# Query products of a hybrid mLSTM and MLA step: rotary parts of four heads in two row-matched tiles, the query norm as a factor per token, sample products last

## The chip, the cores and the metric

The kernel runs on one core of a Trainium2 chip. The metric is the device time of one execution in microseconds (us). Runs of a kernel are compared by the median of their times; beside them stands one execution taken by the hardware profiler, from which all durations below come. Five engines work side by side, each through its own queue of instructions: TensorE (PE, with its weight loads shown as PEld), VectorE (DVE), ScalarE (ACT), GpSimd (POOL) and SyncE (SP, which here only issues DMAs). They meet at semaphores.

## The reference

One step of a decoder trunk of two layers, for 1024 prompt tokens and 8 sample tokens that see 8192 cached positions. Layer 0 mixes with an mLSTM, layer 1 with multi-head latent attention (MLA), and each is followed by a SwiGLU FFN. The change lies in the queries of the MLA layer and in the softmax of its prompt:

```python
c_q, c_kv, k_r = jnp.split(x @ w_in, [Q_LORA, Q_LORA + KV_LORA], axis=-1)
q = (rmsnorm(c_q, g_q) @ w_uq).reshape(B, S, MLA_HEADS, QK_NOPE + QK_ROPE)
q_nope = q[..., :QK_NOPE]                 # 128 of a head's 192 columns
q_rope = rope(q[..., QK_NOPE:], pos)      # the other 64
...
x1, x2 = x32[..., : d // 2], x32[..., d // 2:]
rope = [x1 * cos - x2 * sin, x1 * sin + x2 * cos]
...
s = (scores of q with the keys) * MLA_SCALE
p = jax.nn.softmax(masked s, axis=-1)
```

There are 8 heads, Q_LORA is 384, and x is already multiplied with the RMS factor of the layer's norm. So two factors per token stand in a query: that of the layer's norm (rs in the kernel) and that of the query norm (rq).

## The kernel before, in words

The 1032 tokens lie in the free dimension, in three chunks of 344 (CW); features lie on the partitions. A product in near-float32 precision is three matmuls of "high" and "low" parts (mm3, L131 to L133): high by high, high by low, low by high. So every operand is split (L114, L115): ACT makes the high part, DVE or POOL subtracts it from the source and leaves the low part. Weights come through the pool wp, two buffers each of wr (raw), wh and wl; their high and low parts are lines L114 and L115 too, with the tile names wh and wl. Results of products lie in PSUM tiles sc (four banks) and mm (two); a head's three chunks use sc, sc, mm.

The projections (L1160 on) give c_q in ev_q (L1179 to L1184): DVE multiplies the PSUM tile with rs (L1182, tile cf), ACT squares it for the query norm, and ACT and DVE split it, with g_q as pointer scale, into cqh and cql. rs_of(rq, QL) (L1249) turns the sum of squares into a row of factors over all 128 partitions, with matmuls at L229 and L235, a Newton iteration on DVE and copies on ACT. Then rc, the cosines, and rn, the sines with signs, are multiplied with rq (L1251 on POOL, L1252 on DVE).

queries() follows an order written out by hand, the string ORDER. In it "P3" is plain(3), the 128 unrotated columns of head 3: 27 matmuls over three chunks, each chunk multiplied with rq on DVE (L1334, tile qf), split into qx (the middle chunk's low part on POOL), stored to qn_d by SP (L1339), its eight sample columns copied to qnS (L1341). "R4" is rotary(4), the 64 rotary columns of heads 4 and 5 side by side: 27 matmuls, and ACT copies the result to ra (L1308); then four DMAs on ACT's queue (L1312) write rb, which is ra with the halves of each head exchanged. "t4" is rotate(4): ra times rc on POOL (L1320), rb times rn on DVE (L1321), the sum on DVE (L1322), high parts on ACT (L1325), low parts on DVE (L1326), a store to qr_d per head, and the sample columns to qrS (L1329). "A0" lets the first block of the prompt's attention start. After all of them sample_query() makes sixteen small products of qnS with the absorbed key weights wT (L1377; float32, two records each in the trace).

A scheduler then places all instructions of all engines by data and by its own estimate of when they are ready, and fixes one order per engine, so that neighbouring steps mix: the sample products stand wherever the scheduler found room. Stores of one step are issued when the next has been written.

attention() reads a block's queries back (q from qn_d, qrr from qr_d), and each head's weights w_uk and w_uv as spl (split to swh and swl by ACT and DVE). For a block, PE makes the scores (L1495 to L1502), DVE takes the maximum (L1503) and multiplies it with -SCALE (L1506, L1508), ACT takes the exponential with that as bias and SCALE as a constant scale (L1511), and the rest of the softmax and the products follow. Between prompt blocks stand sixteen units of the samples' attention over the gathered cache (nat and nrp, by POOL).

Of the kernel before, what the change touches and what calls it, by code (L numbers as in the profile page):

```python
# [48 lines left out]
ORDER = "R0 P0 P1 R2 P2 t0 R4 P3 t2 P4 R6 P5 t4 P6 P7 t6 A0"  # L49
# [6 lines left out]
def host_tables():  # L56
    p = np.arange(P)
    c = np.zeros((P, C_END), np.float32)
    c[:, C_ID:C_ID + P] = np.eye(P)
    c[:, C_MM:C_MM + P] = np.where(p[:, None] <= p[None, :], 0.0, BIG)  # L60
    c[:, C_MA:C_MA + P] = np.where(p[None, :] <= p[:, None], 0.0, -BIG)
    c[:, C_SL:C_SL + P] = (p[:, None] % 8) == (p[None, :] % 8)
    c[:, C_MC:C_MC + 2] = (p[:, None] // 64) == np.arange(2)[None, :]
    c[:, C_PM] = p % 16
    c[:, C_L8] = p < 8
    c[:, C_QS:C_QS + 4] = p[:, None] == 32 * np.arange(4)[None, :]
    h = np.arange(8)
# [8 lines left out]
    r = np.stack([np.concatenate([cos, cos, cos, cos]), np.concatenate([-sin, sin, -sin, sin])], 1)  # L76
    return c, r.astype(np.float32)
# [11 lines left out]
class Kern:  # L89
# [39 lines left out]
    def mm3(self, ps, wh, wl, xh, xl, start, stop, **kw):  # L129
        mm = self.nc.tensor.matmul  # L130
        mm(ps, wh, xh, start=start, stop=False, **kw)  # L131
        mm(ps, wh, xl, start=False, stop=False, **kw)  # L132
        return mm(ps, wl, xh, start=False, stop=stop, **kw)  # L133
# [105 lines left out]
    def rms_tok(self, SS, n):  # L239
        nc = self.nc  # L240
        c, rem = divmod(n, P)
        ps = self.tp()
        for i in range(c):
            nc.tensor.matmul(ps[:, i:i + 1], SS[:, i * P:(i + 1) * P], self.ones[:, 0:1], start=True, stop=True)
        v = self.t(self.gp, [P, 9], "tv")
        w = c + (rem > 0)
        if rem:
            nc.gpsimd.memset(v[:, c:w], 1.0)
            nc.tensor.matmul(ps[:rem, c:w], SS[:, c * P:n], self.ones[:, 0:1], start=True, stop=True)
            nc.vector.tensor_scalar(v[:rem, c:w], ps[:rem, c:w], 1.0 / D, EPS, op0=ALU.mult, op1=ALU.add)  # L250
        nc.vector.tensor_scalar(v[:, :c], ps[:, :c], 1.0 / D, EPS, op0=ALU.mult, op1=ALU.add)
        return self.rsqrt(self.gp, v[:, :w], [P, 9], "t", w)
# [856 lines left out]
    def to_mla(self, wd, fs):  # L1109
# [29 lines left out]
        self.as_row(y, rs, T)  # L1139
        return z, rs  # L1140


    def mla(self, z, rs):
# [17 lines left out]
        rq = self.t(cqp, [P, T], "rq")  # L1161
# [4 lines left out]
        rtab = self.t(mt, [P, T], "rtab")  # L1166
# [102 lines left out]
        z = self.attention(ckh, ckl, kk, kl, cqp, (cqh, cql, rc, rn, rq, wT))  # L1269
# [17 lines left out]
    def queries(self, qs, cq):  # L1287
        nc = self.nc
        V = nc.vector
        cqh, cql, rc, rn, rq, wT = cq  # L1290
# [12 lines left out]
        def rotary(h):  # L1303
            ra = self.t(qs, [P, T], "ra", bufs=2)
            rb = self.t(qs, [P, T], "rb", bufs=2)

            def ev(c, cs, ps):
                nc.scalar.copy(ra[:, cs], ps)  # L1308

            self.linear(weights([(i * 64, (h + i) * 192 + P, 64) for i in range(2)]), (cqh, cql), 3, P, ev)  # L1310
            for i in range(4):
                nc.scalar.dma_start(rb[i * 32:i * 32 + 32], ra[(i ^ 1) * 32:(i ^ 1) * 32 + 32])  # L1312
            return ra, rb

        def rotate(h, ra, rb):
            x = [self.t(qs, [P, S], f"qr{i}", F32R, bufs=1) for i in range(2)]
            for c in range(NCH):
                cs = slice(c * CW, (c + 1) * CW)
                w = slice(c * CW, min((c + 1) * CW, S))
                nc.gpsimd.tensor_tensor(ra[:, cs], ra[:, cs], rc[:, cs], op=ALU.mult)  # L1320
                V.tensor_tensor(rb[:, cs], rb[:, cs], rn[:, cs], op=ALU.mult)  # L1321
                V.tensor_tensor(ra[:, cs], ra[:, cs], rb[:, cs], op=ALU.add)  # L1322
                for i in range(2):
                    me, ot = slice(i * 64, i * 64 + 64), slice(64 - i * 64, 128 - i * 64)
                    nc.scalar.activation(x[i][me, w], ra[me, w], AF.Copy)  # L1325
                    V.tensor_tensor(x[i][ot, w], ra[me, w], x[i][me, w].bitcast(F32), op=ALU.subtract)  # L1326
            for i in range(2):
                stores.append(lambda i=i: nc.sync.dma_start(self.qr_d[h + i], x[i].bitcast(F32)))
                V.tensor_copy(self.qrS[:, h + i], ra[i * 64:i * 64 + 64, S:])  # L1329

        def plain(h):
            def ev(c, cs, ps):
                f = self.t(qs, [P, CW], "qf", bufs=3)
                V.tensor_tensor(f, ps, rq[:, cs], op=ALU.mult)  # L1334
# [3 lines left out]
                self.split(x[:, 0], x[:, 1], f[:, :n], lo_eng=nc.gpsimd if c == 1 else None)  # L1338
                stores.append(lambda: nc.sync.dma_start(self.qn_d[h, :, :, w].rearrange("i p s -> p i s"), x.bitcast(F32)))  # L1339
                if n < CW:  # L1340
                    V.tensor_copy(self.qnS[:, h], f[:, n:])  # L1341
# [3 lines left out]
        rot = {}  # L1345
        stores = []
        for op in ORDER.split():
# [56 lines left out]
    def attention(self, ckh, ckl, kk, kl, cqp, cq):  # L1404
# [70 lines left out]
        def prompt(h, G, kt, vt):  # L1475
# [5 lines left out]
            for i in (2 * G, 2 * G + 1):  # L1481
# [8 lines left out]
                for c in range(nb):  # L1490
# [13 lines left out]
                    sc.append((o, ks))  # L1504
                if nb == 2:
                    V.tensor_scalar(mx[:, 0:1], mx[:, 0:1], mx[:, 1:2], -SCALE, op0=ALU.max, op1=ALU.mult)  # L1506
                else:
                    V.tensor_scalar(mx[:, 0:1], mx[:, 0:1], -SCALE, None, op0=ALU.mult)  # L1508
                px = self.t(self.wp, [P, 1024], "wr")
                for c, (o, ks) in enumerate(sc):  # L1510
                    nc.scalar.activation(px[:, ks], o, AF.Exp, bias=mx[:, 0:1], scale=SCALE, accum_out=sm[:, c:c + 1])  # L1511
# [52 lines left out]
        self.sample_query(qs, cq[-1])  # L1564
# [305 lines left out]
```

## Time and profile before

| | us |
|---|---|
| runs | 2786.38, 2792.11, 2802.57 |
| median | 2792.11 |
| the profiled execution | 2765.05 |
| its span, first to last instruction | 2763.3 |
| mean granted PE clock | 0.971 |

In the span, mLSTM, its FFN and the MLA projections come first; the first query product (cqh by wh) starts at 1319.65, the last ends near 1402.5, attention runs until about 1905, and the output projection and the second FFN fill the rest. A row of the profile's groups gives line, engine, operation, output and inputs with their shapes and the count; behind the first bar busy time in us and mean ns of one; behind the second the engine's idle time before these instructions, and what ended it. A row of the waits gives the waiting engine, tile and line, what it waited for, then total us, number of times and the longest. A row of the stretches gives for each engine its busy us and in brackets its instructions, then the granted PE clock, the share of the DMA engines' time, and GB/s. A row of the chain has start, length and what ran.

### The profile page before, as it was taken

Reading aid. Unit: us, or ns where it says so; the run is one execution under the profiler, and the core shown is the slowest. Engines: PE = TensorE matmul, PEld = TensorE weight load, DVE = VectorE, ACT = ScalarE, POOL = GpSimd, SP = SyncE. Lnnn points to the kernel's source line nnn. Section 1 sums busy time; section 2 is a strip of 40 time slices with the busy share of each in tenths; the row PEclk is TensorE's granted clock in tenths of the full one; section 3 lists DMA queues with packets and bytes.
Section 4 is the critical chain, followed back from the end, with each engine's and each line's share of the span. In section 5 each row is a group of like instructions: output and inputs, shape, how many; then the busy total and the mean of one; then the engine's idle time right before and its main releaser. Section 6 shows DMA issues by size and latency. Waiting matters only on the chain.

```text
span 2763.3 us, 52062 instructions
## 1 busy us (share of the span) xinstructions
PE 2587.8 (94%) x20715; PEld 2438.1 (88%) x20715; DVE 1523.6 (55%) x3230; ACT 1181.6 (43%) x2687; POOL 875.2 (32%) x823
## 2 busy tenths in 40 slices
PE   8999998989999999999978878888989999999998
PEld 8998877989999999999866666767888999999998
DVE  4345578863334434465768767676574434434455
ACT  4212334544444444453455544545344444444442
POOL 1001002242333333332335544432223333333333
PEclk9999989999999999999989999998999999999999
DMA  5133455426655565451667765553533655555552
GB/s 184 39 76 92 128 147 134 131 71 126 127 117 117 115 125 116 93 173 54 190 230 272 255 228 194 200 198 119 165 100 90 128 114 123 119 115 117 116 140 100
DMA packets 344346, 378.45 MB, mean 137 GB/s; under 512 B 24250, under 2 KB 297023, under 8 KB 335783
## 3 DMA queue, kind: packets, MB, share of 16 engines
q0 software_dynamic: 37328, 170.42, 26.0%
q1 hardware_dynamic: 289494, 192.07, 23.3%
q10 hardware_dynamic: 17280, 12.64, 2.0%
q8 instruction: 162, 2.65, 0.4%
q14 instruction: 82, 0.66, 0.1%
HBM read 251.44 MB, written 121.51 MB: 135 GB/s over the span
## 4 chain that ended last, share of the span: by engine, by line
PE 66%; DVE 12%; DMA 10%; issue 5%; ACT 4%; POOL 2%; SPq 0%; ACTq 0%; POOLq 0%; DVEq 0%
PE sc L133 10%; PE sc L131 10%; PE sc L132 10%; PE mm L131 5%; PE mm L132 5%; PE mm L133 5%; PE ss L131 5%; PE ss L132 5%; PE ss L133 5%; DMA Gb<-G_d 2%; DVE tt L1648 2%; DVE wl L115 1%; PE ss L1680 1%; DMA nrp<-in_cache_k_rope_dram,idx 1%; PE mm L1552 1%
## 5 line engine op out<-in xcount | busy, mean ns | idle before, releaser
L131 PE MATMUL ss<-ah,dh 128*128 128x344 f32 x864 | 277.1, 321 | 5.9 <-ACT st L1071 5.5
L1071 ACT COPY st<-ss 128x344 f32<-128x344 f32 x432 | 190.0, 441 | 213.3 <-PE ss L133 181.6
L132 PE MATMUL ss<-al,dh 128*128 128x344 f32 x864 | 277.1, 321 | 1.9 <-POOL al L115 1.9
L133 PE MATMUL ss<-ah,dl 128*128 128x344 f32 x864 | 276.4, 320 | 0.0
L114 ACT ACTIVATE wh<-wr 128x512 fp32r<-128x512 f32 (+2 forms) x157 | 126.3, 806 | 230.9 <-PE mm L132 132.6
L1073 POOL DMA_DIRECT2D x_d<-st x144 | 125.2, 869 | 238.4 <-ACT st L1071 235.6
L131 PEld LDWEIGHTS ss<-ah,dh 128*128 128x128 f32 x864 | 162.7, 188 | 6.9 <-ACT st L1071 6.0
L115 POOL TENSOR_TENSOR al<-u,ah 128x512 fp32r<-128x512 f32 (+1 forms) x84 | 118.4, 1410 | 148.5 <-ACT ah L114 148.3
L132 PEld LDWEIGHTS ss<-al,dh 128*128 128x128 f32 x864 | 163.1, 189 | 2.4 <-POOL al L115 2.4
L115 DVE TENSOR_TENSOR wl<-S,wl 128x512 fp32r<-128x512 f32 x89 | 78.0, 877 | 156.9 <-ACT wl L114 122.5
L133 PEld LDWEIGHTS ss<-ah,dl 128*128 128x128 f32 x864 | 162.7, 188 | 0.0
L1648 DVE STREAM_TRANSPOSE tt<-nat 128x1024 f32<-128x1024 f32 x128 | 153.3, 1220 | 16.6 <-PE ss L1655 11.7
L115 DVE TENSOR_TENSOR wh<-S,wh 128x512 fp32r<-128x512 f32 x91 | 68.2, 749 | 120.3 <-ACT wh L114 91.7
L1037 DVE TENSOR_TENSOR u<-u,sc 128x260 f32<-128x260 f32 (+1 forms) x168 | 70.8, 421 | 114.0 <-PE sc L133 112.7
L115 DVE TENSOR_TENSOR wl<-wr,wh 128x1024 fp32r<-128x1024 f32 (+2 forms) x88 | 101.4, 1154 | 31.6 <-ACT wh L114 31.3
L1003 POOL TENSOR_TENSOR S<-S,wr 128x512 f32<-128x512 f32 x45 | 62.9, 1397 | 176.4 <-DVE wl L115 88.4
L996 POOL TENSOR_TENSOR S<-wr 128x512 f32<-128x512 f32 x45 | 62.3, 1385 | 164.8 <-DMA wr<-in_ffn_w_gate_up_dram 159.3
L131 PE MATMUL mm<-zh,wh 128*128 128x344 f32 x320 | 105.3, 329 | 9.1 <-DVE ot L455 9.1
L115 DVE TENSOR_TENSOR dl<-dr,dh 128x256 fp32r<-128x256 f32 x144 | 67.9, 472 | 71.5 <-ACT dh L114 71.5
L132 PE MATMUL mm<-zl,wh 128*128 128x344 f32 x320 | 104.5, 327 | 0.0
L133 PE MATMUL mm<-zh,wl 128*128 128x344 f32 x320 | 104.3, 326 | 0.0
L1005 POOL TENSOR_TENSOR S<-S,wr 128x512 f32<-128x512 f32 x45 | 58.0, 1289 | 129.8 <-DVE wh L115 83.7
(904 smaller groups left out, 9313.5 us busy)
## 6 DMA issues: line engine op xcount, KB each, us to landing
x_d<-st POOLq DMA_DIRECT2D x144, 516.0 KB, 5.5
wr<-in_ffn_w_gate_up_dram SPq DMA_DIRECT2D x98, 512.0 KB
dr<-in_ffn_w_down_dram SPq DMA_DIRECT2D x144, 128.0 KB
wr<-in_mlstm_w_in_dram SPq DMA_DIRECT2D x24, 512.0 KB
wr<-in_mlstm_w_out_dram SPq DMA_DIRECT2D x16, 512.0 KB
q<-qn_d SPq DMA_DIRECT2D x32, 256.0 KB
wr<-in_mla_w_o_dram SPq DMA_DIRECT2D x15, 512.0 KB
qn_d<-qx SPq DMA_DIRECT2D x16, 344.0 KB
```

The lines of the kernel that those rows point to most:

```text
L114: ins = nc.scalar.activation(hi, src, AF.Copy)
L115: self.low = e.tensor_tensor(lo, src, hi.bitcast(F32), op=ALU.subtract)
L131: mm(ps, wh, xh, start=start, stop=False, **kw)
L132: mm(ps, wh, xl, start=False, stop=False, **kw)
L133: return mm(ps, wl, xh, start=False, stop=stop, **kw)
L996: G(s, a21, a22, op=ALU.add)
L1003: G(s, s, a11, op=ALU.subtract)
L1005: G(s, s, a12, op=ALU.subtract)
L1037: V.tensor_tensor(u[:, 1], u[:, 1], ps, op=ALU.add)
L1071: nc.scalar.copy(st[:, cs], ps)
L1073: nc.gpsimd.dma_start(self.x_d[:, d], st, accum_op=ALU.add)
L1648: V.transpose(out=tt, in_=src.rearrange("p s (c i) -> p c s i", i=32))
```

## The change

The query norm's factor isn't applied to the queries of the prompt at all. ev_q splits and squares the PSUM tile directly, without rs. From the sum of squares rms_tok makes, with the layer's factor y, one factor per token in the layout "token on the partition" (rqt, times SCALE and times -SCALE). That is where the softmax needs it: the pointer of the maximum's product and of the exponential's scale takes rqt in place of the constants. For the sample columns, rqS holds the factors as a row, and each evacuation multiplies its eight columns with it.

rotary(h0) now makes four heads at once. Its weights are split so that one product tile holds the first rotary halves of the four heads (32 rows each), and the other the second halves; so x1 and x2 of one head and frequency are in the same row of two tiles, and cosine and sine need no exchange of rows: four multiplications on DVE out of PSUM, a subtraction and an addition on POOL, and the split. The tiles rfa and rfb between them have two buffers. rotate() and its DMAs are gone, the stores to qr_d carry four heads of 32 rows. plain() splits its PSUM tile directly, with all low parts on DVE. ORDER becomes shorter, and sample_query is placed after the last query product. The core of the diff:

```diff
-ORDER = "R0 P0 P1 R2 P2 t0 R4 P3 t2 P4 R6 P5 t4 P6 P7 t6 A0"
+ORDER = "R0 P0 P1 R4 P2 P3 P4 P5 P6 P7 A0"
...
-    def rms_tok(self, SS, n):
+    def rms_tok(self, SS, n, m=D, f=None):
...
+        if f is not None:
+            nc.vector.tensor_tensor(v[:, :w], v[:, :w], f, op=ALU.mult)
+            nc.vector.tensor_scalar(v[:, :w], v[:, :w], EPS, None, op0=ALU.add)
...
-                f = self.t(mt, [P, CW], "cf", bufs=3)
-                V.tensor_tensor(f, ps, rs[:, cs], op=ALU.mult)
-                self.squares(rq[:, cs], f, j == 0)
-                self.split(cqh[:, j, cs], cql[:, j, cs], f, self.gcol(self.G_Q + j))
+                self.split(cqh[:, j, cs], cql[:, j, cs], ps, self.gcol(self.G_Q + j))
+                self.squares(rq[:, cs], ps, j == 0)
...
-        self.rs_of(rq, QL)
-        nc.gpsimd.tensor_tensor(rc, rc, rq, op=ALU.mult)
-        V.tensor_tensor(rn, rn, rq, op=ALU.mult)
+        V.tensor_tensor(y2, self.ry, self.ry, op=ALU.mult)
+        y = self.rms_tok(rq, T, QL, y2)
+        V.tensor_tensor(y, y, self.ry, op=ALU.mult)
+        ps = self.tp()
+        nc.tensor.matmul(ps[:, :NS], y[:, 8:9].to_broadcast([P, P]), self.ident[:, :NS], start=True, stop=True)
+        self.rqS = self.t(p2, [P, NS], "rqS")
+        V.tensor_copy(self.rqS, ps[:, :NS])
+        self.rqt = self.t(p2, [P, 2, 8], "rqt")
+        for i in range(2):
+            V.tensor_scalar(self.rqt[:, i], y[:, 0:8], (SCALE, -SCALE)[i], None, op0=ALU.mult)
...
+        def rotary(h0):
+            raw = self.t(self.wp, [P, KT * P], "wr")[:, : 3 * 256].rearrange("p (k c) -> p k c", c=256)
             for i in range(4):
-                nc.scalar.dma_start(rb[i * 32:i * 32 + 32], ra[(i ^ 1) * 32:(i ^ 1) * 32 + 32])
-            return ra, rb
+                nc.sync.dma_start(raw[:, :, i * 64:i * 64 + 64], self.wsrc(wuq, 0, 3, (h0 + i) * 192 + P, 64))
...
+                for e in range(2):
+                    ps.append(self.mmt(("sc", "mm")[e])[:, :CW])
+                    for k in range(3):
+                        self.mm3(ps[e], wh[:, e, k], wl[:, e, k], cqh[:, k, cs], cql[:, k, cs], k == 0, k == 2)
+                for e, (x, y) in enumerate(((rc, rn), (rn, rc))):
+                    f, g = (self.t(qs, [P, CW], "rf" + i, bufs=2) for i in "ab")
+                    V.tensor_tensor(f, ps[0], x[:, cs], op=ALU.mult)
+                    V.tensor_tensor(g, ps[1], y[:, cs], op=ALU.mult)
+                    nc.gpsimd.tensor_tensor(f, f, g, op=(ALU.subtract, ALU.add)[e])
+                    self.split(out[e][0][:, w], out[e][1][:, w], f[:, :n])
...
         def plain(h):
             def ev(c, cs, ps):
-                f = self.t(qs, [P, CW], "qf", bufs=3)
-                V.tensor_tensor(f, ps, rq[:, cs], op=ALU.mult)
...
-                self.split(x[:, 0], x[:, 1], f[:, :n], lo_eng=nc.gpsimd if c == 1 else None)
+                self.split(x[:, 0], x[:, 1], ps[:, :n])
...
-                    V.tensor_copy(self.qnS[:, h], f[:, n:])
+                    V.tensor_tensor(self.qnS[:, h], ps[:, n:], self.rqS, op=ALU.mult)
...
-                    nc.scalar.activation(px[:, ks], o, AF.Exp, bias=mx[:, 0:1], scale=SCALE, accum_out=sm[:, c:c + 1])
+                    nc.scalar.activation(px[:, ks], o, AF.Exp, bias=mx[:, 0:1], scale=f, accum_out=sm[:, c:c + 1])
...
-        self.sample_query(qs, cq[-1])
+        with self.tc.issue_after(self.lastq.ins):
+            self.sample_query(qs, cq[-1])
```

How the instructions stand on the engines is the scheduler's result. Three places matter.

ACT around the rotary parts of heads 4 and 5. Before, the high parts of a rotation (qr), the copies of the next pair (ra) and the DMAs that swap its halves (rb) stand between the weights' high parts (wh, L114 from wr) and those of plain heads (qx):

```order
1140 L1325 ACTIVATE qr_14786<-ra_14557 64x336
1141 L1308 COPY ra_14686<-sc_14706 128x344
1142 L1325 ACTIVATE qr_14787<-ra_14557 64x336
1143 L114 ACTIVATE wh_14816<-wr_14814 128x384
1144 L1308 COPY ra_14686<-mm_14717 128x344
1145 L1312 DMA rb_14687<-ra_14686 32x1032 x4
1146 L114 ACTIVATE qx_14752<-qf_14750 128x344
```

After, at heads 4 to 7, r0h and r1h are the high parts of the first and the second rotary halves, out of the POOL sums rfa:

```order
1119 L114 ACTIVATE qx_14612<-mm_14602 128x336
1120 L114 ACTIVATE r0h_14630<-rfa_14655 128x344
1121 L114 ACTIVATE r1h_14632<-rfa_14662 128x344
1122 L114 ACTIVATE r0h_14630<-rfa_14689 128x344
1123 L114 ACTIVATE r1h_14632<-rfa_14696 128x344
1124 L114 ACTIVATE r0h_14630<-rfa_14723 128x336
1125 L114 ACTIVATE qx_14766<-sc_14756 128x344
1126 L114 ACTIVATE wh_14802<-wr_14800 128x384
```

The copies to ra and the DMAs have left ACT's queue, and plain heads' high parts read PSUM (sc, mm) in place of qf.

DVE at the same place. Before, the low parts of two weights (wl) stand ahead of a rotation, whose products (rb), sums (ra) and low parts (qr) follow:

```order
1482 L115 TENSOR_TENSOR wl_14692<-wr_14688,wh_14691 128x384
1483 L115 TENSOR_TENSOR wl_14737<-wr_14734,wh_14736 128x384
1484 L1321 TENSOR_TENSOR rb_14558<-rb_14558,rn_13611 128x344 x2
1485 L1322 TENSOR_TENSOR ra_14557<-ra_14557,rb_14558 128x344 x2
1486 L1321 TENSOR_TENSOR rb_14558<-rb_14558,rn_13611 128x344
1487 L1326 TENSOR_TENSOR qr_14786<-ra_14557,qr_14786 64x344
1488 L1326 TENSOR_TENSOR qr_14787<-ra_14557,qr_14787 64x344
```

After, the end of heads 4 to 7 (rfa, rfb, r0l, r1l), with the first chunks of P2 (qx_14766, qx_14779) and the low part of P3's weights (wl_14803):

```order
1497 L1338 TENSOR_TENSOR rfb_14732<-mm_14713,rc_13612 128x344
1498 L115 TENSOR_TENSOR r0l_14631<-rfa_14723,r0h_14630 128x336
1499 L1342 TENSOR_TENSOR rs_14634<-rfa_14723,rqS_14259 128x8
1500 L115 TENSOR_TENSOR qx_14766<-sc_14756,qx_14766 128x344
1501 L1342 TENSOR_TENSOR rs_14634<-rfa_14731,rqS_14259 128x8
1502 L1348 COPY qrS_14391<-rs_14634 32x8 x4
1503 L115 TENSOR_TENSOR r1l_14633<-rfa_14731,r1h_14632 128x336
1504 L1348 COPY qrS_14391<-rs_14634 32x8 x4
1505 L115 TENSOR_TENSOR qx_14779<-sc_14769,qx_14779 128x344
1506 L115 TENSOR_TENSOR wl_14803<-wr_14800,wh_14802 128x384
```

The low part of P3's weights stands behind the last low part of the four heads' rotation; before, the next weights' low parts stood ahead of a pair's rotation.

PE at the sample products (L1377 before, L1392 after). Before, one of them stands between two query heads, with four more places like it, and the last ten behind the scores of the first attention blocks:

```order
8497 L132 MATMUL mm_14538<-cql_13609,wh_14504 128x344
8498 L133 MATMUL mm_14538<-cqh_13608,wl_14505 128x344
8499 L1377 MATMUL ss_15194<-qnS_14402,wT_13613 128x8
8500 L131 MATMUL sc_14566<-cqh_13608,wh_14562 128x344
8501 L132 MATMUL sc_14566<-cql_13609,wh_14562 128x344
```

After, all sixteen stand behind the scores of the first blocks:

```order
8749 L1513 MATMUL sc_15066<-kk_13597,qrr_15046 128x256
8750 L1515 MATMUL sc_15066<-kl_13598,qrr_15046 128x256
8751 L1517 MATMUL sc_15066<-mk_14379 128x128
8752 L1392 MATMUL ss_15106<-qnS_14390,wT_13614 128x8 x16
8753 L1510 MATMUL sc_15211<-kt_14290,q_15205 128x384
```

On PE nothing of the samples stands between query products any more. The scheduler's order of the attention stage that follows differs from before in most rows, on all engines.

More of the change, by code (lines that the diff above doesn't have):

```diff
@@ L132, in mm3 @@
         mm(ps, wh, xl, start=False, stop=False, **kw)
-        return mm(ps, wl, xh, start=False, stop=stop, **kw)
+        self.last = mm(ps, wl, xh, start=False, stop=stop, **kw)
+        return self.last
     def load_w(self, src, nk, m):
@@ L1268, in mla @@
         self.o_d = self.t(self.dp, [P, 8, S], "ot_d")
-        z = self.attention(ckh, ckl, kk, kl, cqp, (cqh, cql, rc, rn, rq, wT))
+        z = self.attention(ckh, ckl, kk, kl, cqp, (cqh, cql, rc, rn, wT))
         for p in (self.to, self.pb, self.pe, self.pq):
@@ L1289, in queries @@
         V = nc.vector
-        cqh, cql, rc, rn, rq, wT = cq
+        cqh, cql, rc, rn, wT = cq
         self.qn_d = self.t(self.dp, [8, 2, P, S], "qn_d")
@@ L1301, in weights @@
             return self.split_w(raw, 3, P)
[L1303 to L1310, printed above, removed]
-            for i in range(4):
-                nc.scalar.dma_start(rb[i * 32:i * 32 + 32], ra[(i ^ 1) * 32:(i ^ 1) * 32 + 32])
-            return ra, rb
@@ L1315, in rotate @@
-        def rotate(h, ra, rb):
-            x = [self.t(qs, [P, S], f"qr{i}", F32R, bufs=1) for i in range(2)]
+        def rotary(h0):
+            raw = self.t(self.wp, [P, KT * P], "wr")[:, : 3 * 256].rearrange("p (k c) -> p k c", c=256)
+            for i in range(4):
+                nc.sync.dma_start(raw[:, :, i * 64:i * 64 + 64], self.wsrc(wuq, 0, 3, (h0 + i) * 192 + P, 64))
+            wh, wl = (self.t(self.wp, [P, KT * P], x, F32R)[:, : 2 * 3 * P].rearrange("p (e k m) -> p e k m", e=2, m=P) for x in ("wh", "wl"))
+            for e in range(2):
+                src = raw.rearrange("p k (h e r) -> p k h e r", e=2, r=32)[:, :, :, e]
+                o = [x[:, e].rearrange("p k (h r) -> p k h r", r=32) for x in (wh, wl)]
+                self.split(o[0], o[1], src)
+            out = [[self.t(qs, [P, S], f"r{e}" + x, F32R, bufs=1) for x in "hl"] for e in range(2)]
+            sm = self.t(qs, [P, 2, NS], "rs", bufs=2)
@@ L1327, in rotate @@
-            for i in range(2):
-                stores.append(lambda i=i: nc.sync.dma_start(self.qr_d[h + i], x[i].bitcast(F32)))
-                V.tensor_copy(self.qrS[:, h + i], ra[i * 64:i * 64 + 64, S:])
+                n = min(CW, S - c * CW)
+                w = slice(c * CW, c * CW + n)
+                ps = []
+                for e in range(2):
+                    ps.append(self.mmt(("sc", "mm")[e])[:, :CW])
+                    for k in range(3):
+                        self.mm3(ps[e], wh[:, e, k], wl[:, e, k], cqh[:, k, cs], cql[:, k, cs], k == 0, k == 2)
@@ L1331, in plain @@
+            for e in range(2):
+                for i in range(2):
+                    r0 = 64 * i + 32 * e
+                    stores.append(lambda e=e, i=i, r0=r0: nc.sync.dma_start(self.qr_d[h0:h0 + 4, r0:r0 + 32], out[e][i].bitcast(F32)))
+                for i in range(4):
+                    V.tensor_copy(self.qrS[32 * e:32 * e + 32, h0 + i], sm[32 * i:32 * i + 32, e])
         def plain(h):
             def ev(c, cs, ps):
-                f = self.t(qs, [P, CW], "qf", bufs=3)
-                V.tensor_tensor(f, ps, rq[:, cs], op=ALU.mult)
@@ L1353, in queries @@
                 plain(h)
-            elif op[0] == "R":
-                rot[h] = rotary(h)
+                self.lastq = self.last
             else:
-                rotate(h, *rot[h])
+                rotary(h)
             for f in due:
```

29 lines of the change are left out of this document (13 added, 16 removed).

## The prediction

> **What bounds the kernel now.** I read the page first, then a table of stretches, the waits of TensorE (PE), the chain, PE's timeline and the groups of instructions. The page, with its span, block 1 and block 4:
>
> ```profile
> span 2763.3 us, 52062 instructions
> PE 2587.8 (94%) x20715; PEld 2438.1 (88%) x20715; DVE 1523.6 (55%) x3230; ACT 1181.6 (43%) x2687; POOL 875.2 (32%) x823
> PE 66%; DVE 12%; DMA 10%; issue 5%; ACT 4%; POOL 2%; SPq 0%; ACTq 0%; POOLq 0%; DVEq 0%
> ```
>
> PE is the bound over most of the span. The change acts where it isn't: in the query products. Four stretches: the first and the second half of these products, the turn to attention, and attention.
>
> ```profile
> core 0: us, PE busy (x) PEld busy (x) DVE busy (x) ACT busy (x) POOL busy (x), PEclk, DMA share, GB/s
> 1319.60:1352.30 32.70, 31.74 (x213) 29.36 (x213) 26.55 (x51) 16.77 (x37) 12.62 (x12) 1.00 0.51 156
> 1352.30:1402.40 50.10, 38.51 (x201) 36.18 (x200) 43.44 (x85) 19.89 (x46) 15.78 (x14) 0.83 0.69 220
> 1402.40:1440.00 37.60, 30.84 (x164) 24.72 (x162) 17.34 (x49) 24.89 (x59) 14.31 (x14) 0.82 0.61 216
> 1440.00:1905.00 465.00, 399.13 (x5044) 316.88 (x5044) 338.03 (x741) 233.66 (x643) 201.17 (x195) 0.94 0.61 215
> ```
>
> In the first half PE is fed (31.74 of 32.70). In the second it idles 11.6 of 50.1 us, its clock falls to 0.83, and VectorE (DVE) is busy 43.44: DVE is what is short there. PE's timeline:
>
> ```profile
> 1319.65 0.32 PE L131 MATMUL sc<-cqh,wh 128*128 128x344 f32 x1
> ...
> 1354.97 0.39 PE L1377 MATMUL ss<-qnS,wT 128*128 128x8 f32 x2 [2.35 <-DVE qnS L1341]
> 1356.50 0.66 PE L131 MATMUL sc<-cqh,wh 128*128 128x344 f32 x1 [1.15 <-ACT wh L114]
> ...
> 1357.99 0.49 PE L131 MATMUL sc<-cqh,wh 128*128 128x344 f32 x1
> ...
> 1362.01 0.49 PE L133 MATMUL sc<-cqh,wl 128*128 128x344 f32 x1
> ...
> 1362.93 0.32 PE L131 MATMUL mm<-cqh,wh 128*128 128x344 f32 x1
> ...
> 1365.92 0.32 PE L132 MATMUL sc<-cql,wh 128*128 128x344 f32 x1
> ...
> 1387.00 0.59 PE L1377 MATMUL ss<-qnS,wT 128*128 128x8 f32 x2 [3.11 <-DVE qnS L1341]
> ...
> 1392.04 0.65 PE L133 MATMUL sc<-cqh,wl 128*128 128x344 f32 x1 [2.35 <-DVE wl L115]
> ...
> 1402.30 0.32 PE L133 MATMUL mm<-cqh,wl 128*128 128x344 f32 x1
> ...
> 1406.64 3.70 PE L1377 MATMUL ss<-qnS,wT 128*128 128x8 f32 x18 [2.53 <-DVE qnS L1341]
> ```
>
> A product's step at full clock is 0.157 us (1362.93 to 1365.92, 19 steps), after the idle time near 1355 it is 0.287 (1357.99 to 1362.01, 14 steps): some 5 to 6 us of half speed, about 3 us lost. The page "TensorE: Matmul & The Clock Gate" of the Trainium skill (Part 1) states half rate after an idle window of about 3.4 us; here 2.35 and 1.15 us with two small products between them were enough, which roughly agrees.
>
> The second half holds 63 of the 108 triples of products:
>
> ```profile
> 1352.30:1402.40 50.10, 22.89 (x63) 13.75 (x63) 0.83 0.69 220
> ```
>
> These 189 products need 29.7 us at 0.157, and took 50.1: **20.4 us** are lost, 11.6 idle and the rest slow clock. PE's waits between 1275 and 1440, and the chain there:
>
> ```profile
> PE ss L1377 <- DVE qnS L1341: 8.5, 4, 3.1
> PE sc L133 <- DVE wl L115: 3.3, 3, 2.3
> PE sc L131 <- ACT wh L114: 3.1, 4, 1.2
> ```
>
> ```profile
> 1353.43 5.87 DMA rb<-ra
> ...
> 1368.82 1.66 ACTq L1312
> ```
>
> PE stops for sample products that stand between query products (L1377), and for the two parts of the next weights, which stand on DVE and ScalarE (ACT) behind a pair's rotation; that rotation waits for its swap through DMA.
>
> **The change part by part.** Prices of one instruction:
>
> ```profile
> L1320 POOL TENSOR_TENSOR ra<-ra,rc 128x344 f32<-128x344 f32 x12 | 13.7, 1168 | 5.5 <-DMA rb<-ra 5.5
> L1326 DVE TENSOR_TENSOR qr<-ra,qr 64x344 fp32r<-64x344 f32 x16 | 8.1, 511 | 0.4
> L1334 DVE TENSOR_TENSOR qf<-sc,rq 128x344 f32<-128x344 f32 x16 | 8.1, 511 | 1.7 <-PE sc L133 1.5
> L1322 DVE TENSOR_TENSOR ra<-ra,rb 128x344 f32<-128x344 f32 x12 | 7.2, 628 | 0.1
> L114 ACT ACTIVATE qx<-qf 128x344 fp32r<-128x344 f32 x16 | 7.4, 486 | 21.5 <-DVE qf L1334 11.9 <-issue 5.4 <-DMA cn_d<-so 2.2
> L117 ACT ACTIVATE cqh<-cf,g 128x344 fp32r<-128x344 f32 x9 | 5.1, 570 | 0.0
> L235 PE MATMUL ss<-rsy,ct 128*128 128x258 f32 x16 | 4.4, 395 | 0.0
> ```
>
> *Norm factor.* The multiplications of cf, rs_of(rq) and the products of rc and rn with rq go; 9-element operations come. All of it lies under a fed PE, so on the path only PE's own records count: half of L235's 4.4 us goes, eighteen one-column products come. I take -1; bounds -2.2 and +1 (were the small ones as long as the large).
>
> *Plain heads.* 24 multiplications qf (0.51 us) leave DVE, eight low parts come to it from POOL (0.51 each): -12.2 + 4.1 = -8.1 us of DVE. ACT keeps its 24 copies. Banks are held until the low part is done, a second instruction; PE's list shows no wait for a bank, so that costs nothing while DVE keeps up.
>
> *Rotary parts.* The products stay (324 in both programs). Per pair DVE now does 3 x 1.25 us of rotation and 6 x 0.51 or more of low parts, near 7 us, 28 for four pairs; after, per four heads, 12 multiplications and 6 low parts, 18 x 0.51 = 9.2, 18.4 for both. The 16 swaps and their issues on ACT's queue go, the 5.87 us flight with them. New is a loop: the buffers rfa and rfb are two each, so a chunk's multiplications wait for the chunk before. One chunk takes a multiplication 0.51, two POOL additions at up to 1.17, a copy 0.49 and a low part 0.51: near 4 us, against 18 x 0.157 = 2.8 of products. A quad's first chunk is read 36 x 0.157 = 5.7 us before its last product, three loops take 12, so its results are complete 6.3 us after that product.
>
> *Where PE stops after.* By the order, three weights are late. R4's low part stands on DVE behind the last evacuations of R0, P0 and P1: R0 is complete 6.3 us after its last product, then come six low parts, small copies and two weights' low parts, 6 x 0.51 + 1 + 2 x 0.51 = 5.1, against 2 x 4.2 that P0 and P1 cover: 6.3 + 5.1 - 8.4 = 3.0. P3's stands behind R4's last low part; P2 covers 27 x 0.157 = 4.2: 6.3 + 1.5 for what else stands ahead on DVE (copies for the samples, a low part of P2) - 4.2 = 3.6. P5's load is issued by SP behind the stores of R4, P2 and P3, 4 x 512 and 6 x 342 KB, 4.1 MB. The fastest stretch of the stage moved 296 GB/s:
>
> ```profile
> 1350.00:1360.00 10.00, 6.41 (x30) 5.79 (x30) 7.68 (x18) 4.04 (x10) 1.54 (x2) 0.79 0.95 296
> ```
>
> So they take 14 us. Counted from R4's last product, the stores start at 6.3 and are through at 20, and P5 is due after P2, P3's stall, P3 and P4, at 3 x 4.2 + 3.6 = 16.2: 4 if it waits for all of these stores, 5 with its split, 2 if a part of the transfers overlaps it. I take 3.5. Sum 10.1. Half clock adds up to 3 each, but while PE is slow DVE catches up, so the one at R4 mostly eats the stall at P3; the one at P5 stays. That makes 10.1 to 13.4; I take **11**, with 8.6 (P5 at 2) and 16.6 (all of it) as the ends.
>
> *Sample products last.* The stops near 1355 and 1387 go (they are in the 20.4). At the end before: 2.53 idle and 3.70 for 18 records; after: 32 records at 0.2 (3.70 / 18) = 6.6, with less of a wait, as one low part and one small product on DVE separate them from the last head. I take +0.5, bounds -2.5 and +3.
>
> *Scale in the exponential.* A pointer in place of a constant. Nearest rows: 570 ns for a copy with a pointer scale, 486 without, so 84 ns more, 91 times by the second row here:
>
> ```profile
> L1511 ACT ACTIVATE wr<-sc,mx 128x512 f32<-128x512 f32 x45 | 30.9, 688 | 18.0 <-DVE mx L1506 15.1 <-PE mm L1532 1.6 <-DVE sm L1514 1.0
> L1511 ACT ACTIVATION_READ_ACCUMULATOR wr<-sc,mx 128x1 f32 x91 | 18.4, 202 | 0.0
> ```
>
> That is 7.6 us of ACT. ACT is busy 233.66 of 465 there, and waits mostly for DVE's maximum; I take +1 on the path, bounds 0 and +7.6. This speaks against the change, and so does the page "ScalarE: Activation LUTs" of the Trainium skill (the paragraph on ACTIVATE under "What ACT_TABLE_LOAD costs"): each pointer operand adds about 93 ns. By that figure it would be an estimated 8.5 us of ACT; the rows' 84 ns agree.
>
> *Attention in a new order.* The scheduler rearranges loads and units of the whole stage. PE's waits from 1440 to 1905 show what such a shift is worth:
>
> ```profile
> PE mm L131 <- ACT swh L114: 12.8, 3, 7.9
> PE sc L1495 <- DMA q<-qn_d: 7.5, 3, 5.9
> ```
>
> One wait more or less is up to 7.9 us. I take 0, bounds -8 and +8.
>
> Sum: -20.4 + 11 - 1 + 0.5 + 1 + 0 = **-8.9 us**. The profiled execution took 2765.05 us (span 2763.3), 1% under the median of the runs, 2792.11. The difference arises in one stage and doesn't scale with the rest, so I set it against the median: 2783. With the stalls at their ends it is -11.3 to -3.3; with attention at its ends too, -19 to +5.
>
> **The rivals.**
>
> *A, PE stays fed.* If POOL's additions are nearer 0.6 us than 1.17 (DVE has more operands in PSUM now, and contends less), the loop drops under PE's 2.8 and the weights are in time. Then -20.4 - 1 + 0.5 + 1 = -19.9: 2772, faster. For it: DVE's sum in the stage falls by some 18 us. Against: P5's load behind the stores doesn't depend on the loop.
>
> *B, the gain is given back in attention.* The exponentials' 7.6 us lie wholly on the path, or one load more is waited for. Then -8.9 + 6.6 to -8.9 + 8, about -1: 2791. For it: blocks whose maximum is waited for 15.1 us in one group. Against: PE is 86% busy there and other units fill in.
>
> *C, slower: loads of attention's weights.* Each head's spl load stands in SP's queue with stores and gathers, and PE then waits for swh: 12.8 / 3 = 4.3 us each now. If the new order exposes six more, that is +25.6 - 8.9 = +17: 2809. It decides from six more at the mean, or three at 7.9 (+15). For it: of twelve such loads three wait now, so there are nine that could.
>
> ```profile
> spl<-in_mla_w_uk_dram SPq DMA_DIRECT2D x8, 128.0 KB
> spl<-in_mla_w_uv_dram SPq DMA_DIRECT2D x4, 256.0 KB
> ```
>
> Against: they'd all have to shift one way.
>
> *D, it doesn't do what it says.* By the order the samples stand last and the swaps are gone. But if the scatter of PE's second half came from the transfers alone (0.95 share above), whose stores all stay, the 20.4 us would come back as waits for loads: 2792.
>
> **How the numbers follow.** A measurement of this kernel can tell about 0.5%, 14 us, from no change. Forecast 0.45, of which 0.12 lies beyond -14 (stalls at the low end with a good draw in attention: -11.3 - 3 or more) and 0.33 within; A 0.25, B 0.15, C 0.12, D 0.03. Faster 0.12 + 0.25 = 0.37; same 0.33 + 0.15 + 0.03 = 0.51; slower 0.12. The range goes down to A with a draw of -8 in attention and 2 for its rounding and the scatter of the runs (2762), and up to B with the scatter that the runs above show above their median, +10 (2801). It leaves out C and the far end of A.
>
> **What would show it.** Right: no rb in the chain, query products over 70 to 76 us instead of 82.8, waits "sc L131 or L133 <- wh or wl" of 8 to 13 us in place of L1377's, DVE some 18 us less busy there, exponentials 60 to 95 ns longer. Wrong: query products in under 65 us (A), PE's waits in attention 15 us above the sum of before (C), or a difference outside 1250 to 1905.

## The result, and the profile after

The changed kernel takes 2813.01 us in the median of six runs (2803.98 to 2818.1), the kernel before 2793.4 on the same chip (2786.38 to 2802.57): ratio 1.0072, 95% interval 1.0053 to 1.0091. It is **slower by 0.7%**, some 20 us, where 9 us less were forecast. The profile of before (2765.05) lies 1% under that kernel's runs beside after's profile (2818.1, span 2816.3), so the 53 us between the two profiles overstate the loss; the ratios, each taken within one session, don't.

The stage of the query products in five stretches, after (us and instructions by engine, then clock, DMA share, GB/s):

```profile
1319.00:1346.00 27.00, 26.66 (x171) 25.85 (x170) 16.99 (x48) 10.37 (x22) 9.66 (x12) 0.87 0.23 62
1346.00:1355.00 9.00, 7.47 (x47) 7.19 (x46) 8.05 (x27) 2.75 (x7) 0.87 (x1) 1.00 0.23 65
1355.00:1380.00 25.00, 11.41 (x58) 10.24 (x56) 7.88 (x21) 4.67 (x11) 4.76 (x7) 0.70 0.53 174
1380.00:1410.00 30.00, 9.94 (x51) 9.65 (x52) 7.98 (x28) 3.26 (x7) 0.00 (x0) 0.67 0.54 182
1410.00:1424.00 14.00, 14.00 (x83) 13.91 (x83) 5.49 (x13) 4.48 (x10) 0.00 (x0) 0.91 0.68 232
```

From 1355 to 1410 TensorE (PE) works 21 of 55 us, and no other engine is busy in its place: VectorE (DVE), which was busy 43 of 50 us there before, is down to 16. PE's timeline has two long stops, and three short ones for the parts of late weights:

```profile
1350.65 0.43 PE L133 MATMUL sc<-cqh,wl 128*128 128x344 f32 x1 [1.53 <-DVE wl L115]
...
1373.21 0.65 PE L131 MATMUL mm<-cqh,wh 128*128 128x344 f32 x1 [11.26 <-DVE rfb L1338]
...
1378.47 0.65 PE L131 MATMUL sc<-cqh,wh 128*128 128x344 f32 x1 [2.31 <-ACT wh L114]
...
1381.88 0.66 PE L133 MATMUL sc<-cqh,wl 128*128 128x344 f32 x1 [1.90 <-DVE wl L115]
...
1409.75 0.66 PE L131 MATMUL sc<-cqh,wh 128*128 128x344 f32 x1 [18.18 <-ACT wh L114]
```

Counted by their products (54 for four rotary parts, 27 for a head), the row at 1350.65 is R4, 1373.21 is the third chunk of P2, 1378.47 and 1381.88 are P3, and 1409.75 is P5. P2's third chunk needs one of the two banks of mm, and both still hold results of R4 that DVE hasn't read (L1338). P5 waits for its weights' high part. What the readers waited for, in the waits of all engines there, and the chain:

```profile
ACT r1h L114 <- DMA qr_d<-r1h: 9.5, 1, 9.5
DVE r1l L115 <- DMA qr_d<-r1l: 9.5, 1, 9.5
ACT qx L114 <- DMA qn_d<-qx: 17.1, 3, 16.1
```

```profile
1348.73 22.11 DMA qr_d<-r1l
...
1384.77 4.73 SPq L1356
1389.60 2.41 SPq L1356
...
1401.22 7.94 DMA wr<-in_mla_w_uq_dram
```

R4's results can't be written because R0's, in the same tiles (one buffer each), haven't been stored: the last store was issued at 1348.73 and landed 22.11 us later. At P5 the chain runs through SyncE (SP), which issues the stores of P2 and P3 from 1384.77 on and the load of P5's weights only behind them, at 1401.22. While little else than these stores was under way (1347 to 1355):

```profile
DMA packets 139, 0.56 MB, mean 70 GB/s; under 512 B 2, under 2 KB 2, under 8 KB 139
q1 hardware_dynamic: 139, 0.56, 24.5%
```

and before, from 1354 to 1357, with its stores of 128 rows and the swaps:

```profile
DMA packets 271, 0.93 MB, mean 311 GB/s; under 512 B 44, under 2 KB 44, under 8 KB 271
```

24.5% of 16 engines is the time of 3.9 engines, and the store's outermost dimension is four heads. The Trainium skill says just that, in "DMA: Bandwidth & Descriptors", the paragraph "How many engines (k)" under "Why a DMA increments its semaphore by 16 and not by 1": a DMA runs on the largest number of engines, at most 16, that divides the slowest dimension above one of both its sides. The trace agrees, and the prediction had not looked at it.

### The profile page after: what moved, and what is told of

Read it like the earlier page. It is cut to its first block, busy times and chain, and to the rows that moved or that the text cites. A ratio compares the mean times of both kernels' runs of the same rounds, so it can differ in the third digit from the quotient of the medians.

```text
span 2816.3 us, 51975 instructions
## 1 busy us (share of the span) xinstructions
PE 2612.3 (93%) x20719; PEld 2450.8 (87%) x20719; DVE 1490.6 (53%) x3213; ACT 1178.3 (42%) x2659; POOL 862.5 (31%) x815
## 4 chain that ended last, share of the span: by engine, by line
PE 67%; DVE 12%; DMA 8%; issue 4%; ACT 4%; POOL 2%; SPq 1%; another core or an unknown queue 1%; POOLq 0%; ACTq 0%; DVEq 0%
PE sc L133 9%; PE sc L131 9%; PE sc L132 9%; PE mm L131 5%; PE mm L132 5%; PE mm L133 5%; PE ss L131 5%; PE ss L132 5%; PE ss L133 5%; PE ss L1697 2%; DVE tt L1665 2%; DMA Gb<-G_d 2%; PE ss L1672 2%; DVE wl L115 1%; PE mm L1568 1%
## 5 line engine op out<-in xcount | busy, mean ns | idle before, releaser
L114 ACT ACTIVATE wh<-wr 128x512 fp32r<-128x512 f32 (+2 forms) x157 | 126.4, 806 | 226.9 <-PE mm L132 131.2
L1672 PE MATMUL ss<-tt,qbd 128*32 128x128 f32 x2560 | 104.9, 296 | 26.4 <-DVE tt L1665 13.5
L1672 PEld LDWEIGHTS ss<-tt,qbd 128*32 128x32 f32 x2560 | 78.4, 118 | 47.9 <-DVE tt L1665 23.1
L1007 POOL TENSOR_TENSOR S<-S,wr 128x512 f32<-128x512 f32 x45 | 62.9, 1398 | 175.7 <-DVE wl L115 87.9
```

Source lines behind the costliest of these rows:

```text
L114: ins = nc.scalar.activation(hi, src, AF.Copy)
L1007: G(s, s, a11, op=ALU.subtract)
L1672: nc.tensor.matmul(psS[32 * j:32 * j + 32, u * P:u * P + P], self.qbd[:, b, cb], tt[:, c, 4 * j:4 * j + 4].rearrange("p s k -> p (s k)"), ...
```

## The experiments

**Theory S**: the shape of the stores to qr_d (4x32x1024) costs the 20 us. **T**: the tiles and DVE's loop do, whatever the store. **Q**: the load of late weights behind the stores in SP's queue does. All ratios are to the kernel before on the chip of the run.

*k1_per_head.* Each store in four, one per head:

```diff
-stores.append(lambda e=e, i=i, r0=r0: nc.sync.dma_start(self.qr_d[h0:h0 + 4, r0:r0 + 32], out[e][i].bitcast(F32)))
+stores.extend(lambda e=e, i=i, r0=r0, j=j: nc.sync.dma_start(self.qr_d[h0 + j, r0:r0 + 32],
+    out[e][i][32 * j:32 * j + 32].bitcast(F32)) for j in range(4))
```

> The changed kernel with each of its eight stores to qr_d issued as four stores of one head, 32 rows of 1024 (128 KB), in place of one store of 4x32x1024. Theory S (the shape of the store): a store whose outermost dimension is 4 runs on few of the 16 DMA engines, 22 us for R0's four stores in the trace of after; per head they spread. Then TensorE's waits of 11.3 us (rfb of R4's first chunks) and 18.2 us (the high part of P5's weights) fall below 3 and 6 us, the DMA share near 1350 goes from 0.15 to 0.35 up to 0.7 or more, the query products end near 1395 to 1400 in place of 1424, and the kernel takes 2785 to 2795 us, ratio to before 0.997 to 1.001. Theory T (tiles: rfa and rfb in two buffers, r tiles in one, whatever the store): the waits stay above 8 and 12 us, 2808 to 2818 us. Theory Q (SP's queue: P5's load stands behind 2 MB of stores in any shape): the first wait goes, the second stays above 12 us, about 2800 us.

Measured: 2779.91 us, ratio 0.9984 (0.9967 to 1.0002): the loss of 0.7% is gone. The same stretch, and PE's longest wait in the stage:

```profile
1346.00:1355.00 9.00, 7.46 (x48) 7.18 (x47) 6.89 (x21) 2.02 (x5) 1.81 (x2) 1.00 0.96 290
```

```profile
PE sc L131 <- ACT wh L114: 14.4, 2, 13.2
```

The DMA share goes from 0.23 to 0.96, and the stops at P2 and at P5 disappear. A stop of 13.2 us stands at P3 instead, where S had said that nothing over 6 would be left. So S holds for the loss, T falls, and Q has a part of its own: ACT waits 9.3 us for a load of weights, which SP issued behind R4's sixteen stores.

```profile
ACT wh L114 <- DMA wr<-in_mla_w_uq_dram: 9.3, 1, 9.3
```

```profile
1369.87 1.78 SPq L1346 DMA_DIRECT2D qr_d<-r1l  x4
1371.70 0.42 SPq L1311 DMA_DIRECT2D wr<-in_mla_w_uq_dram  x1
```

*k2_before_four.* The suspected cost put into the kernel before:

```diff
-self.qr_d = self.t(self.dp, [8, P, S], "qr_d")
+self.qr_d = self.t(self.dp, [4, 4, 2, 32, S], "qr_d")
...
-stores.append(lambda i=i: nc.sync.dma_start(self.qr_d[h + i], x[i].bitcast(F32)))
+stores.append(lambda i=i: nc.sync.dma_start(self.qr_d[h // 2, :, i], x[i].bitcast(F32)))
...
-nc.sync.dma_start(x.bitcast(F32), self.qr_d[h, :, g])
+nc.sync.dma_start(x.bitcast(F32), self.qr_d[h // 2, :, h % 2, :, g])
```

> The kernel before with another layout of qr_d, in which the store of one head's 128 rows is 4x32x1024 with gaps between the four, and the loads of a block read four groups of 32 rows; nothing else differs, and the order of all engines is that of before. Theory S: a pair's two stores take about 10 us on 4 engines in place of 3, the next pair's rotation waits for its tiles and SP's queue for its slots: slower by 8 to 30 us, ratio 1.003 to 1.011, DMA share near 0.25 where only these stores run. Theories T and Q: no change, ratio 0.998 to 1.002.

Measured: 2811.19 us, ratio 1.0091 (1.0066 to 1.0116), as S said. The chain now runs through the stores and what stands behind them:

```profile
1350.91 16.87 DMA qr_d<-qr
1367.85 6.19 DMA wr<-in_mla_w_uq_dram
1375.28 14.79 DMA wr<-in_mla_w_uq_dram
...
1405.40 14.34 DMA qr_d<-qr
```

The shape alone makes the old kernel as slow as the new one. The query products take 100.0 us (1317.22 to 1417.20) in place of some 83, about 17 of the 27 us. The rest lies behind them, where the loads of a block changed with the layout too, so the share of these loads isn't separated.

*k3_two_tiles.* `bufs=2` in place of 1 for r0h, r0l, r1h, r1l, stores as in the change.

> The changed kernel with two buffers in place of one for the tiles r0h, r0l, r1h, r1l, so that R4's results needn't wait for R0's stores; the stores keep their shape of 4x32x1024. Theory S: the wait of 11.3 us at R4 goes, but the stores are as slow and the load of P5's weights as late, so most of it comes back there: 2805 to 2815 us, ratio 1.004 to 1.008. Theory T: 2795 to 2802 us, ratio 1.001 to 1.004, and the wait for P5's weights falls too.

Measured: 2796.97 us, 1.005 (1.0031 to 1.0068). The ratio lies in S's range, but its interval reaches into T's (up to 1.004), and the second buffer may gain a little on the change (1.0053 to 1.0091). The waits decide for S: the stop at P2 goes, and PE waits for weights instead, 14.5 us at P3 and 18.5 at P5, where T had said that the latter falls. In front of these stands ACT, waiting for buffers qx whose stores hang behind those to qr_d.

```profile
PE sc L131 <- ACT wh L114: 33.0, 2, 18.5
ACT qx L114 <- DMA qn_d<-qx: 27.0, 5, 14.6
```

*k4_const_scale.* k1_per_head with `scale=SCALE` and `-SCALE` for f and nf; the query norm's factor is left out of the softmax.

> k1_per_head with the constants SCALE and -SCALE back in the exponential and in the product of the maximum; it leaves the query norm's factor out of the softmax. An exponential costs 60 to 95 ns less on ScalarE. If the path takes most of it: 5 to 8 us under k1_per_head. If other work covers it, as the prediction took: 0 to 2 us, no difference that can be told.

Measured: 2775.99 us, 0.9971 (0.9956 to 0.9987), against 0.9984 (0.9967 to 1.0002): 4 us less, between the two ranges that were expected and with intervals that overlap, so the cost on the path isn't settled. ScalarE's own part is: its 96 exponentials of four widths take 64.6 us in k1_per_head and 55.8 here. One of 128x512, in k1_per_head and here:

```profile
L1527 ACT ACTIVATE wr<-sc,mx,rqt 128x512 f32<-128x512 f32 x45 | 35.1, 781 | 29.2 <-DVE mx L1522 8.8 <-PE mm L1548 8.6 <-PE mm L1568 7.2
```

```profile
L1527 ACT ACTIVATE wr<-sc,mx 128x512 f32<-128x512 f32 x45 | 31.0, 689 | 18.9 <-DVE mx L1524 5.3 <-DVE mx L1522 4.5 <-DVE mx L1518 3.0
```

*k5_own_raw.* k1_per_head with own raw buffers for all query weights:

```diff
-raw = self.t(self.wp, [P, KT * P], "wr")[:, : 3 * P].rearrange("p (k m) -> p k m", m=P)
+raw = self.t(qs, [P, 3 * P], "uw", bufs=8).rearrange("p (k m) -> p k m", m=P)
...
-raw = self.t(self.wp, [P, KT * P], "wr")[:, : 3 * 256].rearrange("p (k c) -> p k c", c=256)
+raw = self.t(qs, [P, 3 * 256], "uz", bufs=2).rearrange("p (k c) -> p k c", c=256)
```

> k1_per_head with buffers of their own for the raw query weights (eight of a plain head, two of four rotary parts), so that SP issues all of their loads ahead of the first store. If the 13.2 us that k1_per_head still waits is the load of P3's weights behind R4's stores in SP's queue, it falls to the 3 to 4 us that DVE's loop leaves, the query products end about 10 us sooner (65 to 72 us from first to last in place of 80), and the kernel takes 8 to 12 us less than k1_per_head: ratio to before 0.993 to 0.996. If DVE's and POOL's loop holds it (the weights' parts stand behind R4's evacuation whatever their load does), nothing changes: 0.997 to 1.000.

Measured: 2756.03 us, ratio 0.9982 (0.9964 to 0.9999), nothing gained over k1_per_head. The products did shrink to 65.0 us from first to last, but began at 1338.48, where b0_before_again on the same chip began at 1317.25; so they ended at 1403.44, no sooner than there (1399.64). The first load was issued at 1320.08, against 1312.73 in k1_per_head; that its new buffer had to wait for memory of the projections isn't shown. The stores then filled all engines (0.97 and 307 GB/s):

```profile
1380.00:1405.00 25.00, 20.57 (x123) 19.77 (x121) 12.57 (x43) 7.57 (x18) 2.34 (x3) 0.93 0.97 307
```

But the first block waited only 1.4 us for its queries. As far as the two traces show, the late beginning took back what the products had gained.

*k8_before_raw.* The same buffers, six of them, in the kernel before.

> The kernel before with six buffers of their own for the raw query weights, nothing else. TensorE's waits there came from the weights' parts behind a rotation on DVE and ACT and from sample products, not from the loads: 0 to -4 us, ratio 0.998 to 1.000. If the loads behind stores matter in this kernel too, -8 to -12 us, and the gain of k5_own_raw is not one of the new rotary form.

Measured: 2768.68 us, 1.0021 (1.0005 to 1.0038): a little slower, outside the expected 0.998 to 1.000, with the same late beginning (1341.9). On the same chip and with a beginning nearly as late, k5_own_raw is 12.7 us faster (2756.03).

*k9_after_raw.* k5's buffers in the changed kernel, stores as in the change.

> The changed kernel with buffers of its own for the raw query weights, its stores to qr_d in the shape 4x32x1024 as they are. Splits the loss of 20 us: the wait of 18.2 us for P5's weights goes, the one of 11.3 us for R4's tiles stays, and R4's and later stores still fill SP's queue: 2793 to 2803 us on the scale of the first measurement, ratio 1.000 to 1.004. If the shape of the stores costs as much by any way (waits for tiles, for blocks read back from qn_d and qr_d), the ratio stays above 1.005.

Measured: 2768.82 us, 1.0025 (1.0006 to 1.0045), in the first range. The stop at P5 is gone, one of 7.2 us stands at P2, and a new one of 9.5 at P6. But its products too begin late, at 1336.9, with other work of PE ahead of them, so it doesn't separate the two causes. k13_late_four keeps the beginning.

*b0_before_again.*

> The kernel before, unchanged, for a second profile, since the one that the prediction used was 1% under the median of the runs. Attention between the last query product and the output projection took 500 us in it; with a time near the median it should take 510 to 520, and the query products 82 to 84 as before.

Measured: 2764.72 us (span 2760.5), where the 29 runs beside it have a median of 2762.0; attention took 500.1 us again (1399.64 to 1899.72), the products 82.4. The expectation of a longer attention missed: on this chip a profile like the first lies near the median. That the first came from as fast a chip would fit, but isn't recorded. By session the same kernel's median was 2762.0, 2783.87, 2784.1, 2786.81 and 2793.4.

*k10_own_late.* k1_per_head with own buffers for heads 3 to 7 alone, so the first loads keep their place:

```diff
-def weights(parts):
-    raw = self.t(self.wp, [P, KT * P], "wr")[:, : 3 * P].rearrange("p (k m) -> p k m", m=P)
+def weights(parts, own=False):
+    raw = (self.t(qs, [P, 3 * P], "uw", bufs=5) if own else
+           self.t(self.wp, [P, KT * P], "wr")[:, : 3 * P]).rearrange("p (k m) -> p k m", m=P)
...
-self.linear(weights([(0, h * 192, P)]), (cqh, cql), 3, P, ev)
+self.linear(weights([(0, h * 192, P)], h >= 3), (cqh, cql), 3, P, ev)
```

> k1_per_head with five raw buffers of their own for the weights of heads 3 to 7 alone. In k5_own_raw the loads of the first weights waited for memory that the projections still held, and the query products began 19 us later (with other products ahead of them); here they begin near 1319 again. If the wait of 13.2 us in k1_per_head is worth its length, the products end near 1387 and the kernel takes 8 to 12 us less than k1_per_head: ratio to before 0.993 to 0.996. If the stores (12.6 MB, 42 us at 300 GB/s) set when the first blocks' queries can be read back, the gain goes to waits for q and qrr behind the last product: 0.997 to 0.999, with a DMA share of 0.9 and more after 1360.

Measured: 2770.38 us against 2784.1, ratio **0.9937** (0.9915 to 0.9959): faster than both kernels, in the first range. The products run from 1316.24 to 1384.35, 68.1 us, and PE's waits for weights, banks and query tiles up to 1450 are small:

```profile
PE sc L131 <- DVE qx L115: 1.7, 1, 1.7
PE sc L1510 <- ACT wr L1527: 1.3, 1, 1.3
PE sc L133 <- DVE wl L115: 1.2, 1, 1.2
```

*k11_before_late.* The same in the kernel before (six buffers, the last two rotary pairs too).

> The kernel before with six raw buffers of their own for the weights of heads 3 to 7 (and of the last two rotary pairs): the same remedy for the old form. Its weights' parts were late on DVE and ACT, not their loads: 0.998 to 1.001. If it gains as much as k10_own_late, the new rotary form and the norm factor are worth nothing here.

Measured: 2781.98 us, 0.9994 (0.998 to 1.0009). The old form gains nothing from early loads; so the gain of k10_own_late belongs to the new form together with them. Measured side by side, the two differ by 11.6 us in their medians, much as k5_own_raw and k8_before_raw did.

*k12_samples_free.* k10_own_late without `issue_after`: four of the sixteen sample products stand between query products.

> k10_own_late with the sample products placed by the scheduler again (four of the sixteen then stand between query products). If they cost what they cost in before, stops of 2 to 3 us each with half clock behind them: 3 to 8 us more than k10_own_late. If their sources are now ready in time (DVE isn't late any more): no difference, 0 to 2 us.

Measured: 2766.08 us, 0.9933 (0.9909 to 0.9957), no difference from k10_own_late that can be told, as expected for sources that are ready in time: PE waits for none of the four. (One stop of 3.1 us at P6, where k10_own_late has 1.7, is for a bank that DVE hasn't read.)

*k13_late_four.* k10_own_late with the stores of the change.

> The changed kernel with the raw buffers of k10_own_late, its stores to qr_d as they are (4x32x1024): the fourth corner beside the changed kernel (1.0072), k1_per_head (0.9984) and k10_own_late (0.9937). If the two faults add up, early loads bring what they brought per head, 0.5%: 1.0025. If the slow stores act mainly by holding up the load of P5's weights, early loads heal most of it: 0.995 to 0.999. If the slow stores act by themselves (tiles of R4, blocks read back), the ratio stays at 1.005 or more.

Measured: 2806.22 us, 1.0063 (1.0047 to 1.0079): the third case, the stores act by themselves. The four corners:

| ratio to before | stores of 4x32 rows | a store per head |
|---|---|---|
| raw weights in shared buffers | 1.0072 (the change) | 0.9984 |
| heads 3 to 7 in own buffers | 1.0063 | 0.9937 |

In k13_late_four the stop at P2 is as long as in the change. The loads are early, and the stop at P5 is gone; but one of 9.4 us stands at P6. The split of its weights stands on ACT behind qx, which waits for a buffer, whose store hangs behind those to qr_d:

```profile
PE mm L131 <- DVE rfb L1338: 11.4, 1, 11.4
PE sc L131 <- ACT wh L114: 10.4, 2, 9.4
```

```profile
ACT qx L114 <- DMA qn_d<-qx: 17.2, 5, 15.3
```

So behind the 18.18 us at P5 in the changed kernel stood two causes at a time, the late load and the late buffer (ACT waits 16.1 us for one there too). Early loads alone moved the stop to P6 and halved it; no run removed the wait for buffers alone. The price of the narrow stores isn't one number either: 0.9% with shared buffers, 1.3% with own ones for heads 3 to 7, but 0.4% between k9_after_raw (1.0025) and k5_own_raw (0.9982). Why it is so small there stays open.

## Why the prediction was wrong

The step that failed is in "Where PE stops after": the stores "take 14 us" at "the fastest stretch", 296 GB/s. It was taken from a stretch whose stores had 128 rows outermost. The new ones have four, and moved 70 GB/s between 1347 and 1355; R0's four alone took 25.3 us, from 1345.54 to 1370.84. Most of what the sum missed follows from it. PE's five stops add up to 35.2 us in place of the 10.1 of the sum, 25 of the 28.5 us between the forecast (-8.9) and the medians (+19.6):

- P2's third chunk: no stop was forecast, 11.3 us came, by R0's stores that hadn't landed. That the r tiles have one buffer each, and so wait for these stores, did not enter the sum.
- P5: 3.5 (2 to 5) were forecast, 18.2 came, by SP's long issuing of stores and by qx buffers that were not free.
- R4's weights: 3.0 were forecast, 1.5 came. P3's: 3.6 were forecast, 4.2 came in two stops, right behind the long one at P2. So the two waits that the sum put down to DVE's loop came to 5.7 for 6.6.
- The products from first to last: 73 us forecast, 105.1 measured (1318.62 to 1423.75). The 22 us over the old 82.7 are about the loss of the runs, 20 us. Attention behind them, up to the samples' output products, took 531.2 us in after's profile, 500.0 in before's and 519.6 in k11_before_late's; what the change adds there can't be told across sessions.

A second thing was missing, which the first hides: the sum asked only for P5's load whether it stands behind stores in SP's queue. With wide stores PE waits 13.2 us at P3 for a load that stands behind R4's stores. Even so, the interval of k1_per_head, -9 to +1 us, just reaches the -8.9 of the sum.

Without these two faults DVE's loop costs less than it was sized at. In k10_own_late, with wide stores and early loads, R4's weights are 1.2 us late, P3 starts after a wait of 0.6, and no stop over 2 us is left within the query products. POOL's additions average 922 to 979 ns in the changed forms, not 1168 (the row is k5_own_raw's). That is the side of rival A, which got 0.25 and the price of -19.9, but not its mechanism: it asked for 0.6 us, and at 0.95 a chunk of the loop still adds up to 3.4 us, over PE's 2.8. Its time is nearly reached by k10_own_late, with products of 68.1 us where A's sign was under 65: 0.63% of 2784.1 are 17.5 us (11 to 24 by the interval; the medians lie 13.7 apart). But k10_own_late has wide stores and early loads, which A didn't speak of.

```profile
L1339 POOL TENSOR_TENSOR rfa<-rfa,rfb 128x344 f32<-128x344 f32 x12 | 10.9, 929 | 31.3 <-DVE rfb L1338 23.3 <-DVE rfa L1337 8.0
```

Of the other steps: of the 20.4 us that PE lost in the second half some 15 could be had (products of 68.1 us in k10_own_late against 83.6 in k11_before_late). DVE is less busy in the stage, as forecast: 46.4 us after, 70.0 before. The norm factor's -1 can't be told: the first product starts between 1316.2 and 1323.2 in the new forms that keep the first buffers, between 1317.2 and 1319.7 in the old ones. "Sample products last" was set at +0.5 and is nothing that can be told (0.9933 against 0.9937). The scale of the exponential was sized at 84 ns from two rows of other shapes; it is 93 (688 to 781). That is also the figure of the Trainium skill's page "ScalarE: Activation LUTs", under "What ACT_TABLE_LOAD costs". The +1 that the sum set for it on the path remains open between 0 and some 9. The upper end of 16.6 for the stalls doesn't come out of its terms (3.0, 3.6 and 5 with three times 3 us of half clock are 20.6); 35 came in any case. Rival C ended on the right side and near the time (2809), but that was luck: waits for swh in attention fell, from 12.8 us in three to 5.6 in two.

```profile
PE mm L131 <- ACT swh L114: 5.6, 2, 3.8
```

No case had slow stores in it, so no term of the sum could reach 2813. It could have been seen by the Trainium skill's rule on the number of engines, or by asking what the new shape had in common with the rows. Four stores of 512 KB at a quarter of 296 GB/s are an estimated 28 us, and R4's first results need R0's tiles some 5 us after R0 is complete (8.4 of P0 and P1, 2.8 of R4's first chunk, less the 6.3 by which R0 is late).

## What to carry to other kernels

Before a DMA's bytes are divided by a bandwidth, look at its outermost dimension on both sides: a store that gathers four heads into one instruction took the time of four engines here, and four instructions of 32 rows each were faster by 0.9% of the whole kernel. A slow store isn't paid where it stands: it is paid by whoever needs its tile again, by the loads behind it in the issuing queue, and by splits that wait for a buffer behind yet another store; so when a remedy for one of these waits doesn't shorten it, look for the second cause. A new form of an operation and the order of loads around it are worth measuring apart: here the new form with wide stores gave nothing that could be told, early loads in the old form gave nothing, and both together gave 0.6%.

## What the runs showed of the hardware

Issuing is held up as well. SP's own rows at the stores of P0 and P1, behind R0's, in the changed kernel and then in k1_per_head (start, time to issue, count):

```profile
1348.73 2.84 SPq L1346 DMA_DIRECT2D qr_d<-r1l  x1
1351.62 17.12 SPq L1356 DMA_DIRECT2D qn_d<-qx  x6
```

```profile
1351.73 5.11 SPq L1356 DMA_DIRECT2D qn_d<-qx  x6
```

R0's last narrow store took 2.84 us to issue, and the six stores behind it 17.12; with wide stores the four of a tile take 1.78 (R4's row above), the six 5.11. So narrow stores cost the queue that issues what follows them, beside the engines that move them.

One kernel's median differed by 1.1% between sessions (2762.0 to 2793.4). In the traces of the old form it is attention that differs, 500.1 us in b0_before_again and 519.6 in k11_before_late, while the products take 82.4 and 83.6; the reason is not known. A comparison of a few per mille holds within one session only.
